# A Strassen FFN on one Trainium2 core: more gate and up pairs by seven products, part of the elementwise work on GpSimd

## The chip, the core and the metric

The kernel runs on one core of one Trainium2 chip. The metric is the device time of one execution in microseconds; three executions of the kernel before took 948.73, 949.64 and 949.51 us (median 949.51). Five engines work side by side, each through its own instructions in order: TensorE (PE, matmuls, with weight loads shown as PEld), VectorE (DVE), ScalarE (ACT), GpSimd (POOL) and SyncE (SP), which here only issues transfers. ACT and POOL issue transfers too, from the same in-order streams as their arithmetic.

## What is computed

Two decoder layers on one sequence of 512 tokens of width 1024, in float32. Each layer is a token mixer (layer 0 a pooling mixer, layer 1 a differential attention), a residual with LayerNorm, a SwiGLU FFN of inner width 2816, and a residual with LayerNorm again:

```python
def _swiglu(x, w_gate, w_up, w_down):
    return (jax.nn.silu(x @ w_gate) * (x @ w_up)) @ w_down

def reference(x, ...):
    for i in range(DEPTH):            # DEPTH = 2
        h = _multiscale_pool(...) if i % 2 == 0 else _diff_attention(...)
        x = _layernorm(ALPHA * x + h, ln_mix_g[i], ln_mix_b[i])
        x = _layernorm(ALPHA * x + _swiglu(x, w_gate[i], w_up[i], w_down[i]), ln_ffn_g[i], ln_ffn_b[i])
    return x
```

The change concerns the gate and up products of both FFNs and the elementwise work around them.

## The kernel before, in words

**Exact products from rounded halves.** TensorE takes its operands in a rounded float32 form. So every operand is cut in two: ScalarE casts it (the high half), VectorE subtracts the cast from the original (the low half, called a low below), and a product is three matmuls: high by high, high by low, low by high. `split` (L107) does this for activations; in the FFN, `advance` (L555 to L577) does it for weights, with the cast at L569 and the low at L572.

**Weights.** All weights lie in DRAM in rows of 128x1024 (512 KB). `fetch` (L95) and `refill` have SyncE load them into five raw buffers; `advance(upto)` casts and subtracts ahead of the products, into six pairs of weight buffers. The steps of this work are listed by hand per pair (L528 to L545).

**The gate stage.** The inner width is 22 blocks of 128, taken as eleven pairs (k, k + 11). A *plain* pair multiplies gate and up weights of both blocks with all 512 tokens: 4 weight rows, 96 matmuls of 512 columns. A *Strassen* pair (`SPLIT`, pairs 4 to 10; `strassen`, L778) sees the pair as a 2x2 product of halves (tokens by halves of the 1024 input features) and makes seven half-size products P1, Q5, P6, Q3, P7, P2, Q4 instead of eight: 24 matmuls of 256 columns each. It needs sums of weight rows (four per pair, VectorE, L566), and sums of x (`xs`, made once by `sums_of_x`, L604). The products accumulate in three PSUM banks A, B and C of eight; between products ScalarE copies or VectorE subtracts from a bank (L829 to L849), and the result is `hid`, the gated hidden activations.

**Start of the gate stage.** Before both halves of the tokens are normalised and transposed, the first blocks (three in layer 0, two in layer 1) are multiplied with tokens 0 to 255 alone, then with tokens 256 to 511. `turn(n, s)` (L234), the transposition of token block s, runs in between; `late` says where.

**Down sums.** The down product is Strassen too. It needs sums of down weight rows: `load_terms` (L658) has GpSimd's queue load a block and add one row to it in flight (the accumulating transfer, L666), `sum_terms` (L669) adds twice on VectorE (128x512 each, L671 and L672) and stores `tsum` through ScalarE's queue. It also needs sums of `hid`: `sum_hidden(k)` (L691) has four additions of 128x256 on VectorE (L697 to L700), a cast on ScalarE (L702), a low of 128x512 on VectorE (L704), and a store `ssum` through ScalarE's queue. Such generators are put in the list `behind`, and `catch_up()` takes one step of each after every product. `affine` (L203) applies the LayerNorm's gain and bias to the residual rows (two VectorE operations of 128x1024 for each of four token blocks).

Nothing is scheduled by a tool: each engine's order is the order of the calls.

Of the kernel before, what the change touches and what calls it, by code (L numbers as in the profile page):

```python
# [12 lines left out]
F32 = mybir.dt.float32  # L13
# [3 lines left out]
ALU = mybir.AluOpType  # L17
# [31 lines left out]
SPLIT = (4, 5, 6, 7, 8, 9, 10)  # L49
# [5 lines left out]
def trunk(ctx, tc, x, wall, pscale, lam_p, subln, table, lng, lnb, band, first, onehot, out):  # L55
# [37 lines left out]
    total = wall.shape[0]  # L93

    def fetch(upto):  # L95
        while fetched[0] < min(upto, total):
            c = fetched[0]
            raws[c] = keep.tile([P, 1024], F32, tag="raw", name=f"raw{c}", bufs=RAWS)
            nc.sync.dma_start(out=raws[c], in_=wall[c])
            fetched[0] += 1  # L100
# [133 lines left out]
    def turn(n, s):  # L234
        transposed(n, s)
        turned(n, s)
# [226 lines left out]
    def ffn(layer, late):  # L463
        n = 2 * layer + 1
        final = n == 2 * DEPTH - 1
        c0 = base[0]
        c1 = c0 + 2 * FB
        tt = nc.vector.tensor_tensor
        with tc.tile_pool(name=f"ffn{layer}", bufs=1) as fp:
# [7 lines left out]

            order = [k + j * HALF for k in range(HALF) for j in range(2)]
# [3 lines left out]
            def block(i, b):  # L482

                if PAIRS[i][1] == 2:
                    return wall[c1 + 4 * i + b]
                return wall[c1 + 20 + b // 2][:, (b % 2) * 512 : (b % 2 + 1) * 512]
# [32 lines left out]

            chunks, index, steps = [], {}, []  # L520
# [7 lines left out]
            for k in range(HALF):  # L528
                j0 = index[k] = len(chunks)
                c = c0 + 4 * k  # L530
                if k in SPLIT:

# [3 lines left out]
                    for w in (  # L536
                        "low 0, sum 1, cast 1, sum 4, cast 3, cast 4, low 1, sum 2, cast 2, low 3, "
                        "low 2, sum 6, cast 5, cast 6, low 4, low 5, low 6"
                    ).split(", "):
                        steps.append((w[:-2], j0 + int(w[-1])))  # L540
                else:
                    for i in range(4):
                        chunks.append((c + i, ()))
                        step("cast", j0 + i)
                        step("low", j0 + i)  # L545
# [11 lines left out]
            def advance(upto, strict=False):  # L557

                upto = min(upto, len(chunks))
                while not all(j in finished for j in range(upto)):  # L560
                    kind, j = steps.pop(1 if strict and steps[0][1] >= upto else 0)
# [8 lines left out]
                    else:  # L570
                        h, l = halves[j]
                        tt(l, t, h.bitcast(F32), op=ALU.subtract)  # L572
# [32 lines left out]

            def sums_of_x():

                r0, r1, r2, r3 = spare(4), spare(15), spare(6), spare(17)

                def whole(t, a, b):  # L610
                    tt(t, quarter(a, 0, b).bitcast(F32), quarter(a, 1, b).bitcast(F32), op=ALU.add)
# [7 lines left out]
                whole(r2, 0, 0)  # L619
                yield  # L620
                whole(r3, 0, 1)
                yield
                whole(r0, 1, 0)
                whole(r1, 1, 1)
                yield
# [3 lines left out]
                high(2, r0)  # L629
                yield  # L630
                tt(r2, r1, r2, op=ALU.subtract)  # L631
                high(1, r2)
                low(0, r1)
# [3 lines left out]
                low(2, r0)  # L637
                yield
# [12 lines left out]

            def load_terms(k):
                if k < HALF - 1:
                    c = c1 + 4 * (k // 2)
                    src = wall[c : c + 4][:, :, term_slice(k)].rearrange("(j r) p t -> p j r t", j=2)
                else:
                    src = wall[c1 + 20 : c1 + 22].rearrange("j p (r t) -> p j r t", r=2)
                if k == 1:  # L658
                    t = rows_of[:, :, 4:6, :]
                elif k % 2 == 0 and k < HALF - 1:  # L660
                    t = rows_of[:, :, 9:11, :]
                else:
                    t = keep.tile([P, 2, 2, 512], F32, tag="gb", name=f"b{layer}_{k}")
                for j in range(2):
                    nc.gpsimd.dma_start(out=t[:, j], in_=src[:, j])  # L665
                nc.gpsimd.dma_start(out=t[:, 0], in_=src[:, :, 1], accum_op=ALU.add)  # L666
                terms[k] = t

            def sum_terms(k):  # L669
                t = terms.pop(k)  # L670
                tt(t[:, 1, 1], t[:, 0, 0], t[:, 1, 1], op=ALU.add)  # L671
                tt(t[:, 1, 0], t[:, 1, 1], t[:, 1, 0], op=ALU.add)  # L672
# [4 lines left out]
                if k + 2 < HALF - 1 and k != 1:  # L677
                    load_terms(k + 2)
                if k == HALF - 2:
                    load_terms(HALF - 1)  # L680

            summed_rows = [0]
            behind = []

            def weight_sums():
                g = sum_terms(summed_rows[0])
                summed_rows[0] += 1
                next(g)
                behind.append(g)

            def sum_hidden(k):  # L691
# [8 lines left out]
                tt(u[:, 1, :], u[:, 1, :], second, op=ALU.add)  # L700
# [676 lines left out]
```

## Time and profile before

One profiled execution has a span of 947.3 us from the first to the last instruction, beside the runs' median of 949.51 us.

| what | value |
|---|---|
| span of the profiled execution | 947.3 us |
| PE busy | 934.1 us, 99% |
| DVE busy | 781.3 us, 82% |
| ACT busy | 490.1 us, 52% |
| POOL busy | 108.4 us, 11% |
| PE's share of the chain that ended last | 92% |
| first product of layer 0's gate stage to the first down product | 32.36 to 266.67 us |
| the same in layer 1 | 603.27 to 833.82 us |
| bytes moved | 196.99 MB, mean 208 GB/s |

An engine's row of a timeline gives the start, the time of one instruction (of several equal ones, x2, together), the engine, the line, the operation with output and inputs, and in brackets what it had waited for. Successive instructions overlap a little in it, so that the distance between two starts is the better price of one in a dense stretch. A row of the table by stretches gives each engine's busy time in it, the clock granted to TensorE, the busy share of the transfer engines and what they moved.

### The profile page before, as it was taken

The page shows a single profiled execution, that of the slowest core. Times are in us where ns is not written, and L with a number is a line of the kernel's source. Part 1 is how long each engine was busy: PE and PEld are TensorE (multiplying, and loading weights), DVE is VectorE, ACT ScalarE, POOL GpSimd, SP SyncE. Part 2 cuts the span into 40 slices and gives each one's busy share as a digit, 9 for nine tenths or more (in the row PEclk, how much of TensorE's full clock was granted, in tenths as well). Part 3 has the DMA queues.
Part 4 walks back from the last instruction along what each step waited for, and adds up shares of the span by engine and source line. Part 5 has one row for each costly group of instructions (what it writes and reads, how often), then busy time and mean ns, then how long its engine had stood idle before and what let it go on. Part 6 is the DMA issues. An engine that isn't in the chain of part 4 may idle for free.

```text
span 947.3 us, 15363 instructions
## 1 busy us (share of the span) xinstructions
PE 934.1 (99%) x5976; PEld 845.7 (89%) x5976; DVE 781.3 (82%) x1149; ACT 490.1 (52%) x788; POOL 108.4 (11%) x133
## 2 busy tenths in 40 slices
PE   9999999999999999999999999999999999999996
PEld 8898899999988888988888888998899999988885
DVE  8859879999988777688777677789779999987778
ACT  6752444555564457655566553833345554564450
POOL 4121121110001101000000000211111110001101
PEclk9999999999999999999999999999999999999998
DMA  9387988885888964333233222396888885878952
GB/s 244 125 266 236 341 269 246 265 261 208 255 255 271 363 219 136 95 89 101 78 123 83 64 90 90 118 324 197 262 266 250 255 272 204 261 249 271 356 171 90
DMA packets 82248, 196.99 MB, mean 208 GB/s; under 512 B 14804, under 2 KB 26324, under 8 KB 82174
## 3 DMA queue, kind: packets, MB, share of 16 engines
q1 hardware_dynamic: 42876, 115.07, 36.9%
q0 software_dynamic: 15520, 46.14, 17.8%
q10 hardware_dynamic: 23778, 34.78, 10.2%
q8 instruction: 47, 0.77, 0.3%
q14 instruction: 27, 0.22, 0.1%
HBM read 159.25 MB, written 36.72 MB: 207 GB/s over the span
## 4 chain that ended last, share of the span: by engine, by line
PE 92%; DVE 4%; ACT 2%; issue 1%; POOL 0%; DVEq 0%; POOLq 0%
PE A L820 17%; PE P L886 13%; PE C L820 9%; PE Q L886 6%; PE B L820 4%; PE g L129 3%; PE u L128 3%; PE u L127 3%; PE u L129 3%; PE g L127 3%; PE g L128 3%; PE s L1085 2%; PE v L127 2%; PE v L128 2%; PE v L129 2%; PE q L128 2%
## 5 line engine op out<-in xcount | busy, mean ns | idle before, releaser
L566 DVE TENSOR_TENSOR raw<-raw,raw 128x1024 f32<-128x1024 f32 x56 | 68.3, 1219 | 0.5
L109 ACT CAST xs<-hid 128x512 fp32r<-128x512 f32 (+1 forms) x60 | 34.7, 581 | 24.4 <-DVE hid L734 24.4
L224 ACT ACTIVATE y<-pt,bT,gT 128x128 f32<-128x128 f32 x96 | 36.1, 456 | 20.1 <-PE pt L213 20.1
L110 DVE TENSOR_TENSOR xs<-hid,xs 128x512 fp32r<-128x512 f32 (+1 forms) x60 | 38.5, 644 | 7.8 <-ACT xs L109 7.8
L1095 ACT ACTIVATE p<-p,mn 128x128 f32<-128x128 f32 (+3 forms) x64 | 35.4, 554 | 14.9 <-DVE mn L1090 14.9
L665 POOL DMA_DIRECT2D b<-in_wall x20 | 14.0, 705 | 175.0 <-DVE g_58l L572 66.1
L598 DVE TENSOR_TENSOR hid<-sg,u 128x512 f32<-128x512 f32 x16 | 11.0, 687 | 27.5 <-PE u L129 16.8
L726 POOL DMA_DIRECT2D xs<-ssum x24 | 17.4, 725 | 140.7 <-PE Q L886 119.5
L177 POOL TENSOR_TENSOR rs<-rs,mhalf 128x1 f32<-128x1 f32 x16 | 12.5, 784 | 170.5 <-DVE rs L176 131.0
L110 DVE TENSOR_TENSOR xt<-y,xt 128x512 fp32r<-128x512 f32 x24 | 16.3, 689 | 17.5 <-ACT xt L109 17.5
L1090 DVE CUSTOM_DVE_ANT_0 p<-s,bias 128x128 f32<-128x128 f32 (+3 forms) x64 | 28.1, 485 | 0.0
L665 POOL DMA_DIRECT2D hid<-in_wall x24 | 18.7, 821 | 81.1 <-DMA tsum<-hid 49.4
L110 POOL TENSOR_TENSOR sql<-sq,sqh 128x512 fp32r<-128x512 f32 x7 | 9.0, 1291 | 165.3 <-ACT sqh L109 165.3
L702 ACT CAST v<-u 128x512 fp32r<-128x512 f32 x22 | 13.6, 620 | 26.9 <-DVE u L700 26.7
L168 DVE BATCH_NORM_STATS2 st<-res 128x6 f32<-128x512 f32 x32 | 22.2, 695 | 1.1
L846 ACT ACTIVATE sg<-sg 128x512 f32<-128x512 f32 x14 | 8.9, 633 | 25.7 <-DVE sg L839 25.7
L110 DVE TENSOR_TENSOR heads<-k,heads 128x512 fp32r<-128x512 f32 x8 | 5.5, 692 | 19.9 <-ACT heads L109 19.9
L614 ACT CAST xs<-hid 128x1024 fp32r<-128x1024 f32 x8 | 8.4, 1051 | 24.0 <-DVE hid L631 11.6
L666 POOL DMA_DIRECT2D hid<-in_wall x12 | 14.8, 1232 | 48.2 <-DMA hid<-in_wall 44.9
L835 DVE TENSOR_TENSOR hid<-C,hid 128x512 f32<-128x512 f32 x14 | 9.7, 692 | 10.8 <-PE C L820 9.2
L1109 DVE SCALAR_TENSOR_TENSOR p<-p,sm,p 128x128 f32<-128x128 f32 (+3 forms) x32 | 17.7, 552 | 1.1
L109 ACT CAST heads<-k 128x512 fp32r<-128x512 f32 x8 | 4.7, 589 | 26.0 <-PE k L129 26.0
(1119 smaller groups left out, 3727.7 us busy)
## 6 DMA issues: line engine op xcount, KB each, us to landing
raw<-in_wall SPq DMA_DIRECT2D x122, 512.0 KB, 4.5
r<-tsum SPq DMA_DIRECT2D x40, 512.0 KB, 4.3
hid<-in_wall POOLq DMA_DIRECT2D x36, 512.0 KB, 6.9
b<-in_wall POOLq DMA_DIRECT2D x30, 512.0 KB, 6.4
r<-in_wall SPq DMA_DIRECT2D x30, 512.0 KB, 4.5
tsum<-hid ACTq DMA_DIRECT2D x24, 512.0 KB, 5.3
ssum<-v ACTq DMA_DIRECT2D x22, 512.0 KB, 4.4
tsum<-b ACTq DMA_DIRECT2D x20, 512.0 KB, 5.2
```

The costliest lines, as they stand in the source:

```text
L109: nc.scalar.copy(dst_h, src)
L110: (low or nc.vector).tensor_tensor(dst_l, src, dst_h.bitcast(F32), op=ALU.subtract)
L127: nc.tensor.matmul(acc, ah, bh, start=start, stop=False)
L128: nc.tensor.matmul(acc, ah, bl, start=False, stop=False)
L129: nc.tensor.matmul(acc, al, bh, start=False, stop=stop)
L224: nc.scalar.activation(y[:, k, :], pt[:, k * P : (k + 1) * P], AF.Identity, bias=bT[:, n, kk : kk + 1], scale=gT[:, n, kk : kk + 1],)
L566: tt(t, raws[pair[0]], raws[pair[1]], op=ALU.add)
L665: nc.gpsimd.dma_start(out=t[:, j], in_=src[:, j])
L820: nc.tensor.matmul(o, w[:, c], x[:, kk, :], start=p in ("P1", "Q5", "P2") and f + kk + e == 0, stop=p in ("Q4", "Q3", "P2") and (f, kk, e) ...
L886: nc.tensor.matmul(accs[s], x[:, k, r], y[:, c], start=first and k == 0 and e == 0, stop=last and k == m - 1 and e == 2, skip_group_check= ...
L1090: nc.vector.tensor_tensor_reduce(out=p, in0=accs[c][:, :w], in1=biases[h][:, w - 1 :: -1] if w < S else biases[h][:, ::-1], op0=ALU.add, o ...
L1095: nc.scalar.activation(p, p, AF.Exp, bias=mn[:, q, c : c + 1], scale=-1.0, accum_out=sm[:, q, c : c + 1],)
```

## The change

Ten of the eleven pairs are made by Strassen's scheme; pair 0 alone stays plain. Layer 0 starts with the products P1 and P2 of pairs 1, 2 and 3 (layer 1: pairs 1 and 2), which need only the first token half. These stay in their banks A and B. Then comes plain pair 0, then the started pairs (five products left) in turn with others (seven). Started pairs load their weight rows 0 and 3 twice. `slow`, GpSimd's tensor_tensor, makes now: both additions of each down weight sum, all five operations of `sum_hidden`, both operations of the FFN's four affine steps, the two sums of x over the first token half, and one low of 128x1024 in each started pair and in those others with an index up to 6 (layer 1: up to 4). The two sums of x over the second token half go away: `turn` writes its float32 result there. The accumulating transfer is issued later than the loads it follows.

```diff
-SPLIT = (4, 5, 6, 7, 8, 9, 10)
+SPLIT = tuple(range(1, HALF))
+EARLY = (3, 2)
...
+    def sequence(layer):
+        early = EARLY[layer]
+        first, others = range(1, early + 1), range(early + 1, HALF)
+        return [k for p in zip(first, others) for k in p] + list(others)[early:]
...
-    def turned(n, s):
+    def turned(n, s, kept=None):
         for i, pt in enumerate(turns.pop((n, s))):
-            y = keep.tile([P, 4, P], F32, tag="y", name=f"y{n}_{s}_{i}", bufs=2)
+            if kept:
+                y = kept[i][:, :, s % 2 * P : (s % 2 + 1) * P]
+            else:
+                y = keep.tile([P, 4, P], F32, tag="y", name=f"y{n}_{s}_{i}", bufs=2)
...
+        slow = nc.gpsimd.tensor_tensor
...
+                if k in started:
+                    chunks += [(c, (c, c + 1)), (c, (c, c + 2)), (c + 2, ()), (c + 1, (c + 1, c + 2))]
+                    chunks += [(c, (c, c + 3))]
+                    listed(
+                        j0,
+                        "sum 0, cast 0, cast 2, sum 3, cast 3, low 0, sum 1, cast 1, low 2, "
+                        "low 1, sum 4, cast 4, low 3, low 4",
+                    )
+                    slow_lows |= {j0 + 2}
...
+                    if k <= 2 * early:
+                        slow_lows |= {j0 + 5}
...
-                        tt(l, t, h.bitcast(F32), op=ALU.subtract)
+                        (slow if j in slow_lows else tt)(l, t, h.bitcast(F32), op=ALU.subtract)
...
             def sum_terms(k):
+                for _ in range(4 if k == HALF - 1 else 0):
+                    yield
                 t = terms.pop(k)
-                tt(t[:, 1, 1], t[:, 0, 0], t[:, 1, 1], op=ALU.add)
-                tt(t[:, 1, 0], t[:, 1, 1], t[:, 1, 0], op=ALU.add)
+                slow(t[:, 1, 1], t[:, 0, 0], t[:, 1, 1], op=ALU.add)
+                slow(t[:, 1, 0], t[:, 1, 1], t[:, 1, 0], op=ALU.add)
+                yield
                 yield
                 dst = tsum[:, k // 2, :, term_slice(k)].rearrange("(j r) p t -> p j r t", j=2)
                 for j in range(2):
                     nc.scalar.dma_start(out=dst[:, j], in_=t[:, j])
...
+                yield
+                yield
+                load_terms(following)
+                yield
+                yield
+                yield
+                add_terms(following)
...
-                tt(u[:, 0, :], first, second, op=ALU.subtract)
-                tt(second, second, a22, op=ALU.subtract)
-                tt(u[:, 1, :], a12, first, op=ALU.subtract)
-                tt(u[:, 1, :], u[:, 1, :], second, op=ALU.add)
+                slow(u[:, 0, :], first, second, op=ALU.subtract)
+                slow(second, second, a22, op=ALU.subtract)
+                slow(u[:, 1, :], a12, first, op=ALU.subtract)
+                slow(u[:, 1, :], u[:, 1, :], second, op=ALU.add)
+                yield
                 yield
                 nc.scalar.copy(v[:, :, 0, :], u)
                 yield
-                tt(v[:, :, 1, :], u, v[:, :, 0, :].bitcast(F32), op=ALU.subtract)
+                slow(v[:, :, 1, :], u, v[:, :, 0, :].bitcast(F32), op=ALU.subtract)
...
+            def pool_work():
+
+                def whole(t, b):
+                    slow(t, quarter(0, 0, b).bitcast(F32), quarter(0, 1, b).bitcast(F32), op=ALU.add)
+
+                whole(r2, 0)
+                yield
+                whole(r3, 1)
+                yield
+                add_terms(0)
+                for s in range(SB):
+                    z, gb = res[:, s, :], gbs[n - 1]
+                    slow(z, z, gb[:, 0, :], op=ALU.mult)
+                    yield
+                    slow(z, z, gb[:, 1, :], op=ALU.add)
+                    if s == 1:
+                        add_terms(1)
+                    yield
+
             load_terms(0)
             load_terms(1)
+            side = pool_work()
+            e = 0
+            for k in started:
+                for p in ("P1", "P2"):
+                    b = "A" if p == "P1" else "B"
+                    banks[k, b] = bank(f"{b}{layer}_{k}")
+                    part(banks[k, b], e, p)
+                    if e in late:
+                        turn(n - 1, late[e], (r0, r1))
+                    ahead(e + 6)
+                    next(side, None)
+                    e += 1
...
+            def plain(k):
+                j = index[k]
+                for f in (k, k + HALF):
+                    a = (bank(f"g{layer}_{f}"), bank(f"u{layer}_{f}"))
                     for i in range(2):
+                        product(a[i], j, 0, S)
+                        j += 1
+                        next(sums, None)
+                        ahead(j + 5)
+                        next(side, None)
+                        next(side, None)
                         catch_up()
+                    gated(f, *a)
+                    if f == k:
+                        behind.append(sum_terms(1))
+                behind.append(sum_hidden(k))
...
+            next(sums)
+            behind.append(sum_terms(0))
+            plain(0)
+            for g in (sums, side):
+                for _ in g:
+                    pass
+            for i, k in enumerate(pairs):
+                strassen(k, i + 2)
...
-    ffn(0, {(0, 1): later(0, 2), (1, 0): later(0, 3)})
-    attention(later(1, 3))
-    ffn(1, {(0, 1): later(2, 3)})
+    ffn(0, {1: 2, 2: 3})
+    attention(lambda: turn(1, 3))
+    ffn(1, {0: 2, 1: 3})
```

More of the change, by code (lines that the diff above doesn't have):

```diff
@@ L515, in refill @@
                     held[0] += 1
+            started = list(range(1, early + 1))
+            pairs = sequence(layer)
             chunks, index, steps = [], {}, []
@@ new lines, in strassen @@
+            def strassen(k, following):
+                names = {"P1": "A", "P6": "A", "P7": "A", "Q4": "A", "Q5": "C", "Q3": "C", "P2": "B"}
+                pair = hid[:, k : k + HALF + 1 : HALF, :]
+                first, second = pair[:, :, :256], pair[:, :, 256:]
+                todo = [p for p in GATE if k not in started or p not in ("P1", "P2")]
+                for j, p in enumerate(todo):
+                    if (k, names[p]) not in banks:
+                        banks[k, names[p]] = bank(f"{names[p]}{layer}_{k}")
+                    flat = banks[k, names[p]]
+                    part(flat, index[k] + j, p)
+                    acc = both(flat)
+                    if p == "P1" or j == 0:
+                        g0 = tile_of(k, 0)
+                        nc.scalar.copy(g0, banks[k, "A"])
+                    if k in started and j == 0:
+                        tt(g0, banks[k, "B"], g0, op=ALU.add)
+                    if p == "Q5":
```

241 lines of the change are left out of this document (98 added, 143 removed).

## The prediction

> **What bounds the kernel now.** I read the page first, then busy time by stretches, then the chain that ended last.
>
> ```profile
> span 947.3 us, 15363 instructions
> PE 934.1 (99%) x5976; PEld 845.7 (89%) x5976; DVE 781.3 (82%) x1149; ACT 490.1 (52%) x788; POOL 108.4 (11%) x133
> ```
>
> ```profile
> core 0: us, PE busy (x) PEld busy (x) DVE busy (x) ACT busy (x) POOL busy (x), PEclk, DMA share, GB/s
> 66.00:86.00 20.00, 20.00 (x110) 17.41 (x110) 19.73 (x23) 4.71 (x7) 2.69 (x3) 1.00 1.00 314
> 165.88:186.04 20.16, 20.16 (x170) 20.16 (x170) 19.18 (x24) 10.33 (x13) 2.83 (x4) 1.00 0.93 281
> ```
>
> TensorE is the bound: 99% of the span. The second stretch is one Strassen pair. TensorE never stops, but VectorE is busy 19.18 of 20.16 us and stays just hidden. More Strassen pairs mean less TensorE and more VectorE work; so the question is what GpSimd's help is worth.
>
> ```profile
> 128.43 2.88 PE C L820 x24
> ...
> 266.67 14.99 PE P L886 x66
> 281.66 14.96 PE Q L886 x66
> ...
> 833.82 14.99 PE P L886 x66
> ```
>
> In the chain a product of 24 matmuls of 256 columns takes 2.88 us (0.120 each); 66 matmuls of 512 columns take 14.96 (0.2267 each, not 0.240). So a Strassen pair costs 7 x 2.88 = 20.16, a plain one 96 x 0.2267 = 21.76. The gate stages end at 266.67 and 833.82; they begin here:
>
> ```profile
> 32.36 0.38 PE L127 MATMUL g<-xt,w2h 128*128 128x256 f32 x1 [0.39 <-ACT xt L109]
> ...
> 53.69 0.28 PE L127 MATMUL g<-xt,w2h 128*128 128x256 f32 x1
> ```
>
> ```profile
> 603.27 0.36 PE L127 MATMUL g<-xt,w100h 128*128 128x256 f32 x1
> ```
>
> They last 234.3 and 230.6 us.
>
> **The change, part by part.** *TensorE.* The program has 528 more matmuls of 256 columns and 336 fewer of 512: 528 x 0.120 - 336 x 0.2267 = 63.4 - 76.2 = -12.8 us. A gate stage then needs 10 x 20.16 + 21.76 and two transpositions of about 1.0, 225.4 us. This is all that the change can win.
>
> *Banks in layer 0.* Three started pairs hold six of eight banks; block 0's gate and up take the last two, so block 11's gate waits for block 0's silu. In ScalarE's order two casts stand ahead of that silu, and the first writes a weight buffer that block 0's up product reads to its end.
>
> ```profile
> 52.55 1.28 ACT L597 ACT_TABLE_LOAD   x1
> ...
> 56.77 0.60 ACT L597 ACTIVATE sg<-g 128x512 f32<-128x512 f32 x1 [2.94 <-PE g L129]
> 57.26 1.04 ACT L569 CAST g_6h<-raw 128x1024 fp32r<-128x1024 f32 x1
> ```
>
> TensorE stops for 2 x 1.04 + 1.28 + 0.60 = 4.0 us. Pair 1's first product waits in the same way for a cast and block 11's silu, 1.6. Layer 1 holds four banks and has no such wait. Together +5.6, if nothing longer covers it.
>
> *Work moved to GpSimd.* First VectorE's prices, from a dense part of the Strassen pair, then GpSimd's.
>
> ```profile
> 169.07 0.68 DVE L849 TENSOR_TENSOR hid<-sg,hid 128x512 f32<-128x512 f32 x1
> 169.68 0.69 DVE L671 TENSOR_TENSOR hid<-hid 128x512 f32<-128x512 f32 x1
> ...
> 173.73 1.22 DVE L572 TENSOR_TENSOR g_36l<-raw,g_36h 128x1024 fp32r<-128x1024 f32 x1
> 174.87 1.22 DVE L572 TENSOR_TENSOR g_37l<-raw,g_37h 128x1024 fp32r<-128x1024 f32 x1
> 176.00 0.69 DVE L704 TENSOR_TENSOR v<-u,v 128x512 fp32r<-128x512 f32 x1
> ```
>
> From start to start: 0.60 for 128x512, 1.135 for 128x1024.
>
> ```profile
> 9.85 2.55 POOL L110 TENSOR_TENSOR xt<-res,xt 128x512 fp32r<-128x512 f32 x2 [7.02 <-ACT xt L109]
> 13.90 1.80 POOL L110 TENSOR_TENSOR xt<-res,xt 128x512 fp32r<-128x512 f32 x1 [1.50 <-ACT xt L109]
> 16.32 3.45 POOL L110 TENSOR_TENSOR w2l<-raw,w2h 128x1024 fp32r<-128x1024 f32 x1 [0.61 <-ACT w2h L109]
> ```
>
> ```profile
> 13.32 1.22 DVE L110 TENSOR_TENSOR pw0l<-raw,pw0h 128x1024 fp32r<-128x1024 f32 x1
> 14.46 1.28 DVE L110 TENSOR_TENSOR pooled<-pool,pooled 128x512 fp32r<-128x512 f32 x2
> ...
> 16.25 1.23 DVE L110 TENSOR_TENSOR pw1l<-raw,pw1h 128x1024 fp32r<-128x1024 f32 x1
> 17.39 0.69 DVE L161 SCALAR_TENSOR_TENSOR res<-res,mix 128x512 f32<-128x512 f32 x1
> ```
>
> Undisturbed, GpSimd takes 1.275 for 128x512. The one at 13.90 took 0.53 more: VectorE was in a subtraction with both inputs in SBUF, and GpSimd's end, 15.70, is 1.24 after VectorE had left it (14.46). The one at 16.32 ended at 19.77, 2.38 after VectorE went on from such a subtraction (17.39). While VectorE read one input from PSUM (pool, mix), GpSimd was not held. So GpSimd stands still while VectorE reads two SBUF inputs. Undisturbed prices: 2.38 for 128x1024, and for 128x256, which the trace lacks, 0.72 on the line through both sizes (half of 1.275, 0.64, is the lower bound).
>
> Is VectorE held too while GpSimd works? The nearest rows are an attention operation (L1105) beside GpSimd's low.
>
> ```profile
> 416.66 1.29 POOL L110 TENSOR_TENSOR sql<-sq,sqh 128x512 fp32r<-128x512 f32 x1 [37.94 <-ACT sqh L109]
> ```
>
> ```profile
> 398.39 0.35 DVE L1105 TENSOR_SCALAR p<-p,sm,nlam 128x128 f32<-128x128 f32 x1
> 417.61 0.42 DVE L1105 TENSOR_SCALAR p<-p,sm,nlam 128x128 f32<-128x128 f32 x1
> ```
>
> ```profile
> L1105 DVE TENSOR_SCALAR p<-p,sm,nlam 128x128 f32<-128x128 f32 x8 | 3.3, 412 | 0.3
> ```
>
> Free of GpSimd it takes 0.35. Begun beside GpSimd's low it takes 0.42 and ends at 418.03, 0.08 after GpSimd (417.95). The mean of the eight, 0.412, says that most were late so. It has one SBUF input, so it is kin, not proof: between "not held" and "held until GpSimd ends" I take the second, which its end agrees with.
>
> The Trainium skill ("SBUF — State Buffer", section "Who interferes with whom") states that a VectorE instruction with two SBUF inputs and a GpSimd instruction that reads SBUF exclude each other, for the whole instruction, whoever came first. By that rule moving such work wins nothing and makes it twice as dear; the trace agrees on GpSimd's side (3.45 instead of 2.38), and no run here shows the other side for two inputs. With the page's rule alone the sum below stays as it is.
>
> Then both engines' work of this kind adds up. Per gate stage, layer 0 (layer 1):
> - VectorE: 64 (66) lows, 40 weight sums, 8 operations for the sums of x, 112 (114) x 1.135; 20 gatings and 4 lows of x, 24 x 0.60: 141.5 (143.8).
> - GpSimd: 2 sums of x, 8 affine, 6 (4) lows, 16 (14) x 2.38; 22 down sums and 11 lows of hidden sums, 33 x 1.275; 44 additions x 0.72: 111.9 (107.1).
>
> Sum 253.4 (250.9), against 225.4 of TensorE. VectorE's operations on PSUM, 32 x 0.60, run beside GpSimd and are not counted. Queueing makes it a bound: ScalarE's stores of down sums wait for GpSimd's additions, and behind them in ScalarE's order stand the casts and bank copies that TensorE needs; GpSimd's lows feed TensorE directly. So GpSimd can lag by about one pair: its last hidden sum and down sum, 4 x 0.72 + 3 x 1.275 = 6.7, may fall after the stage. Changing hands costs VectorE the overlap of two instructions, 1.22 - 1.135 = 0.09, at up to 93 (91) operations; I take half, 4.2, as some fall where VectorE waits anyway.
>
> In layer 0 GpSimd begins where it did, with the down loads that follow the pool stage:
>
> ```profile
> 46.40 1.60 POOL L665 DMA_DIRECT2D hid<-in_wall  x2 [4.47 <-ACT xt L109]
> ```
>
> Layer 0 ends at 46.4 + 253.4 - 6.7 + 4.2 = 297.3, 30.6 later; layer 1 takes 250.9 - 6.7 + 4.2 = 248.4 from 603.27, 17.8 longer. The bank wait is covered. 947.3 + 30.6 + 17.8 = 995.7, and the runs' median, 949.51, lies 2.2 above the span of 947.3: 998.
>
> *The rest.* A pair moves ten transfers of 512 KB, 5.2 MB; a started and another pair (34.6 us) 303 GB/s, under the 314 of the first stretch above: nothing. Late loads have about a pair of slack.
>
> **Rivals.** *B, the engines do not hold each other for long:* VectorE runs on. GpSimd has 112 us of work and its issues,
>
> ```profile
> L665 POOL DMA_DIRECT2D hid<-in_wall x24 | 18.7, 821 | 81.1 <-DMA tsum<-hid 49.4 <-DVE g_36l L572 9.5 <-DVE u L700 8.3
> L666 POOL DMA_DIRECT2D hid<-in_wall x12 | 14.8, 1232 | 48.2 <-DMA hid<-in_wall 44.9 <-DMA raw<-in_wall 3.3
> ```
>
> 22 x 0.82 + 11 x 1.23 = 32, 144 of 225. Its first down sum, which ScalarE needs before block 11's silu at 79.4 (53.69 + 4 x 5.44 + 4.0), is ready at 46.4 + 4 x 0.82 + 4.8 + 1.2 + 9.5 + 1.2 + 2.4 + 4.8 + 2.6 = 76.2: in time. Then 947.3 - 12.8 + 5.6 + 2.2 = 942. For it: POOL is busy 11% now, so the time is there. Against: the 3.45 and the 0.42. It decides as soon as VectorE's 128x1024 stay at 1.22 beside GpSimd. *C, one-sided:* GpSimd waits out each VectorE instruction in flight, VectorE is never held. The ten operations before that down sum are late by up to 1.14 each; ScalarE stalls by up to 8 in layer 0 and 6 in layer 1: 942 to 956, middle 949. For it: 13.90 and 16.32 show just this side. Against: 0.42.
>
> **How the numbers follow.** A has 0.65, B 0.21, C 0.14. A's own range: with 0.64 for 128x256 (3.5 a layer) and no changing of hands (4.2), 983; with all of it (4.2) and 5% of each sum idle, as VectorE was in the dense pair (12.6), 1031. The whole range reaches down to B's 942 plus 1, and up to 1025: 943 to 1025 leaves out half of B and A's top. Under 0.2%, 1.9 us, is no change that a measurement of this kernel can tell. Faster: B and 0.03 of C, 0.24; same 0.05 of C; slower: A and 0.06 of C, 0.71.
>
> **What would show it.** Right: in the gate stages VectorE's 128x1024 take well over 1.22 and GpSimd's well over 2.38, their spans alternate, TensorE waits for lows and for ScalarE behind its stores, and the stages last about 265 and 248. Wrong: VectorE's groups keep their means, TensorE's idle time is a few us around plain pair 0 in layer 0, and the stages last about 230 and 225. In both, a Strassen product must keep 2.88.

## The result, and the profile after

The changed kernel takes 1056.92 us (median; 1055.69 to 1058.19) beside 949.58 for the kernel before on the same chip: ratio 1.1131, 95% interval 1.1115 to 1.1147. Slower was forecast, 998 us; the range ended at 1025. The profiled execution has a span of 1056.1 us, 108.8 more than before.

First the page of the changed kernel: span, busy time by engine, and the granted clock in 40 slices.

```profile
span 1056.1 us, 15912 instructions
PE 952.6 (90%) x6168; PEld 868.3 (82%) x6168; DVE 843.0 (80%) x1021; ACT 517.8 (49%) x824; POOL 419.9 (40%) x317
PEclk9985998999999999999999999896989999999999
```

TensorE has 12.8 us less to do (forecast: 934.1 - 12.8 = 921.3) and yet is busy for 952.6: 31.3 us more, in matmuls at a lower granted clock (0.956 on average, 0.997 before). Idle time grew from 947.3 - 934.1 = 13.2 to 1056.1 - 952.6 = 103.5 us. So -12.8 + 31.3 + 90.3 = 108.8. Where it stands, by the chain that ended last (a product of 24 matmuls, and the first down product of each layer):

```profile
119.61 2.88 PE A L816 x24
...
330.05 14.99 PE P L953 x66
...
942.44 14.99 PE P L953 x66
```

A product that nothing disturbs still takes 2.88 us. Layer 0's down stage begins at 330.05 in place of 266.67, 63.4 us later; layer 1's at 942.44 in place of 833.82, a further 45.2. The rest of the kernel is as long as before. Within the gate stages, busy times and granted clock by stretches (start, pair 1's first product, the end of the interleaved pairs, the last four pairs; then layer 1's start):

```profile
core 0: us, PE busy (x) PEld busy (x) DVE busy (x) ACT busy (x) POOL busy (x), PEclk, DMA share, GB/s
32.40:116.50 84.10, 48.78 (x262) 41.52 (x261) 67.27 (x44) 33.40 (x52) 49.95 (x27) 0.78 0.46 148
116.50:242.00 125.50, 108.69 (x840) 107.47 (x840) 96.14 (x79) 52.45 (x68) 87.59 (x63) 0.93 0.77 231
242.00:330.00 88.00, 84.75 (x697) 83.94 (x698) 75.28 (x68) 43.90 (x57) 47.61 (x35) 1.00 0.71 224
667.00:720.00 53.00, 38.23 (x209) 33.64 (x208) 50.86 (x28) 21.01 (x33) 39.64 (x20) 0.88 0.45 129
```

The start is worst: TensorE works 48.78 of 84.10 us, at 0.78 of its clock. In the last stretch it is nearly whole again.

Is VectorE held by GpSimd? Timelines of the two engines in the same microseconds, VectorE first:

```profile
77.03 3.43 DVE L619 TENSOR_TENSOR g_10l<-raw,g_10h 128x1024 fp32r<-128x1024 f32 x1
80.38 3.35 DVE L663 TENSOR_TENSOR hid<-hid 128x1024 f32<-128x1024 f32 x1
```

```profile
79.31 3.33 POOL L838 TENSOR_TENSOR res<-res,gb 128x1024 f32<-128x1024 f32 x1
```

VectorE's 128x1024 take 3.4 us instead of 1.22, GpSimd's 3.33 instead of 2.38. They start alternately, and each instruction's time holds most of one of the other's. VectorE's reads of a bank are not held (group by line, the bank read at 686 ns as before, the weight sums at 1611 ns instead of 1219):

```profile
L613 DVE TENSOR_TENSOR raw<-raw,raw 128x1024 f32<-128x1024 f32 x80 | 128.9, 1611 | 4.2 <-DMA raw<-in_wall 3.2
L902 DVE TENSOR_TENSOR hid<-C,hid 128x512 f32<-128x512 f32 x20 | 13.7, 686 | 29.0 <-PE C L816 26.1
```

The turns are not always one by one. At the start of layer 1, GpSimd's timeline and one VectorE low beside it:

```profile
670.30 2.91 POOL L707 DMA_DIRECT2D hid<-in_wall  x4 [0.25 <-PE pt L232]
673.24 4.84 POOL L829 TENSOR_TENSOR hid<-xt 128x1024 f32<-128x1024 f32 x2
...
678.81 2.79 POOL L838 TENSOR_TENSOR res<-res,gb 128x1024 f32<-128x1024 f32 x1
```

```profile
671.95 10.74 DVE L129 TENSOR_TENSOR w109l<-raw,w109h 128x1024 fp32r<-128x1024 f32 x1
```

One subtraction stood from 671.95 to 682.69 while GpSimd issued transfers and ran three operations, and TensorE waited for it. What TensorE waited for in the whole kernel (microseconds in total, times, longest):

```profile
PE A L816 <- DVE hid L904: 36.2, 20, 4.9
PE g L146 <- ACT sg L644: 23.7, 1, 23.7
PE g L147 <- DVE xt L129: 9.6, 2, 8.5
...
PE B L816 <- DVE w109l L129: 5.7, 1, 5.7
```

Neither of the two largest is in the sum that gave 998: Q4 waits until VectorE has read P7's bank (L904), which the forecast doesn't have, and block 11's gate waits for block 0's silu (L644) to free a bank, 23.7 us where 4.0 was forecast and held to be covered. ScalarE's timeline while TensorE stands, from 77.3 to 101.0 us:

```profile
83.77 1.04 ACT L658 CAST xs<-hid 128x1024 fp32r<-128x1024 f32 x1 [5.52 <-DVE hid L663]
87.05 1.04 ACT L658 CAST xs<-hid 128x1024 fp32r<-128x1024 f32 x1 [2.24 <-DVE hid L666]
91.52 1.04 ACT L616 CAST g_11h<-raw 128x1024 fp32r<-128x1024 f32 x1 [3.42 <-DVE raw L613]
98.02 1.05 ACT L658 CAST xs<-hid 128x1024 fp32r<-128x1024 f32 x1 [5.46 <-DVE hid L670]
```

These four casts stand ahead of that silu, and each waits for a sum that VectorE has yet to make (three sums of tokens, one of weight rows).

### The profile page after: what moved, and what is told of

Same layout as the page of the kernel before. It is cut to its first block, busy times and chain, and to the rows that moved or that the text cites. A ratio compares the mean times of both kernels' runs of the same rounds, so it can differ in the third digit from the quotient of the medians.

```text
span 1056.1 us, 15912 instructions
## 1 busy us (share of the span) xinstructions
PE 952.6 (90%) x6168; PEld 868.3 (82%) x6168; DVE 843.0 (80%) x1021; ACT 517.8 (49%) x824; POOL 419.9 (40%) x317
## 3 DMA queue, kind: packets, MB, share of 16 engines
q0 software_dynamic: 15520, 46.14, 16.4%
## 4 chain that ended last, share of the span: by engine, by line
PE 62%; DVE 21%; issue 6%; ACT 4%; DMA 2%; ACTq 0%; DVEq 0%; POOL 0%; POOLq 0%; SPq 0%
PE A L816 16%; PE P L953 12%; PE C L816 8%; DVE raw L613 6%; PE Q L953 6%; PE s L1152 2%; PE v L146 2%; PE v L147 1%; PE v L148 1%; DMA raw<-in_wall 1%; PE q L147 1%; PE q L148 1%; PE q L146 1%; PE k L146 1%; PE k L148 1%
## 5 line engine op out<-in xcount | busy, mean ns | idle before, releaser
L613 DVE TENSOR_TENSOR raw<-raw,raw 128x1024 f32<-128x1024 f32 x80 | 128.9, 1611 | 4.2 <-DMA raw<-in_wall 3.2
L744 POOL TENSOR_TENSOR u<-hid 128x256 f32<-128x256 f32 x22 | 34.4, 1562 | 72.8 <-DVE hid L916 72.7
L752 POOL TENSOR_TENSOR v<-u,v 128x512 fp32r<-128x512 f32 x22 | 43.4, 1974 | 13.7 <-ACT v L750 13.7
L707 POOL DMA_DIRECT2D hid<-in_wall x32 | 24.9, 787 | 32.1 <-DMA tsum<-hid 26.7
L902 DVE TENSOR_TENSOR hid<-C,hid 128x512 f32<-128x512 f32 x20 | 13.7, 686 | 29.0 <-PE C L816 26.1
L246 ACT ACTIVATE y<-pt,bT,gT 128x128 f32<-128x128 f32 x64 | 24.1, 455 | 17.4 <-PE pt L232 17.3
L745 POOL TENSOR_TENSOR hid<-hid 128x256 f32<-128x256 f32 x22 | 30.8, 1399 | 2.2 <-DVE hid L645 0.6
L900 ACT COPY hid<-A 128x512 f32<-128x512 f32 x20 | 11.7, 587 | 38.9 <-PE A L816 36.6
L712 POOL DMA_DIRECT2D hid<-in_wall x16 | 19.7, 1228 | 26.5 <-DMA hid<-in_wall 18.3
L719 POOL TENSOR_TENSOR hid<-hid 128x512 f32<-128x512 f32 x16 | 29.2, 1825 | 1.3
L909 ACT ACTIVATE sg<-A 128x512 f32<-128x512 f32 x20 | 11.7, 587 | 35.6 <-PE A L816 35.6
L746 POOL TENSOR_TENSOR u<-hid 128x256 f32<-128x256 f32 x22 | 29.0, 1318 | 0.0
L718 POOL TENSOR_TENSOR hid<-hid 128x512 f32<-128x512 f32 x16 | 27.0, 1690 | 0.0
L913 ACT ACTIVATE sg<-sg 128x512 f32<-128x512 f32 x20 | 12.6, 631 | 27.3 <-DVE sg L906 27.3
L146 PE MATMUL g<-xt,g_8h 128*128 128x512 f32 x8 | 4.5, 559 | 23.7 <-ACT sg L644 23.7
```

What stands on the lines that cost most here:

```text
L146: nc.tensor.matmul(acc, ah, bh, start=start, stop=False)
L613: tt(t, raws[pair[0]], raws[pair[1]], op=ALU.add)
L719: slow(t[:, 1, 0], t[:, 1, 1], t[:, 1, 0], op=ALU.add)
L744: slow(u[:, 0, :], first, second, op=ALU.subtract)
L745: slow(second, second, a22, op=ALU.subtract)
L752: slow(v[:, :, 1, :], u, v[:, :, 0, :].bitcast(F32), op=ALU.subtract)
```

## The experiments

Three theories stood. T: the engines exclude each other where both read SBUF, and the added load is the whole loss. R1: ScalarE's queue, stores ahead of casts and silus. R2: banks and the order of the products. R3, a merely slow GpSimd, had fallen with the 3.4 us rows above. In the tables, each ratio is to the kernel before on the same chip, with its 95% interval.

**1. Back to VectorE, at once and part by part**

```diff
-        slow = nc.gpsimd.tensor_tensor
+        slow = nc.vector.tensor_tensor
```

(everything; in the other three `slow` becomes `tt` at L619 alone, at L829, L838 and L840, or at L718 to L752.)

> Ten Strassen pairs as in the changed kernel, but everything that was moved to GpSimd is back on VectorE. Theory T (GpSimd's reads and VectorE's two-operand instructions take turns, so their work adds; the rest of the loss, starved sums and the lower granted clock, follows from that): with GpSimd idle VectorE carries about 216 us in a gate stage beside TensorE's 225, so TensorE sets the end again: 936 to 960 us, granted clock back to 0.99, TensorE busy near 921. Rival R1 (ScalarE's queue: stores that wait for sums hold up the silus and casts behind them, whoever makes the sums): 990 to 1030. Rival R2 (six banks held through the first products in layer 0 and the bank that each Strassen pair reuses; nothing to do with who adds): at least 1010 us, with the first-products stretch of layer 0 still 80 us long. Rival R3 (GpSimd is only slow, and its results come late; no shared path): like T in the time, but then in the part-by-part runs VectorE's own instructions would keep their 1.14 us.

> As the changed kernel, but the ten 128x1024 lows that GpSimd makes are back on VectorE; the other GpSimd work stays. T: by the prices of the added load, 10 x (2.38 - 1.135) = 12.4 us leave the sum, and a low that TensorE waits for is no longer made by an engine with a queue of other work, so 1030 to 1045 us. R1 and R2: no change beyond 5 us (1052 to 1062). R3: 1020 to 1045.

> As the changed kernel, but the quarter sums and the affine steps at the start of each FFN (20 instructions of 128x1024) are back on VectorE. T: 20 x (2.38 - 1.135) = 25 us leave the sum, and with nothing in a row on GpSimd no VectorE instruction is starved beyond one of GpSimd's, so the first-products stretch of layer 0 (84 us) comes down by 12 to 20 and the whole time to 1005 to 1032. If only the sum counts and no starving: 1030. R1, R2: 1050 to 1060. R3 (VectorE gets 22.7 us more, TensorE waits as long): 1050 to 1080.

> As the changed kernel, but the down weights' sums and the sums of the gated hidden (seven instructions for each of 22 pairs) are back on VectorE; GpSimd keeps the lows, the quarter sums and the affine steps. T: of the added load 22 x (6.7 - 3.1) = 79 us go, more than what lies above TensorE in the steady stretch, so TensorE sets the end there and the loss of the start stays: 970 to 1000 us. R1: 1000 to 1030 (the stores still wait for sums, sooner made). R2: 1040 or more. R3: 975 to 1010.

| on VectorE | us | less than 1056.9 | ratio |
|---|---|---|---|
| everything | 1000.89 | 56.0 | 1.0540 (1.0524 to 1.0556) |
| lows | 1044.49 | 12.4 | 1.1004 (1.0988 to 1.1021) |
| start (sums of x, affine) | 1032.52 | 24.4 | 1.0879 (1.0852 to 1.0906) |
| sums of down weights and hidden | 1035.47 | 21.4 | 1.0894 (1.0871 to 1.0917) |

The parts add up: 12.4 + 24.4 + 21.4 = 58.2 beside 56.0. Lows and start give just what 1.135 instead of 2.38 an instruction promised (12.4 and 25). The sums gave 21 of 79, and 1035.47 lies in no theory's range (T: 970 to 1000). In the pairs most of the added load seems to lie under TensorE's own work. Layer 0's last four pairs in the chain that ended last, first in the changed kernel, then with everything on VectorE:

```profile
242.01 6.02 PE A L816 x48
```

```profile
216.63 5.84 PE A L816 x48
...
300.80 14.99 PE P L953 x66
```

They take 88.0 us (242.01 to 330.05) with GpSimd and 84.2 without, 3.9 of the 29.3 us by which this layer's gate stage differs.

T missed the first run too: with GpSimd out of it, 1001 and not 936 to 960. R2 (at least 1010) missed as well, though part 2 finds what it names among the losses. R1's 990 to 1030 holds this run, but not the lows and the start, for which it had 1050 and more; part 4 tries it by itself. About half of the loss is not the shared path. TensorE's waits with everything on VectorE:

```profile
PE A L816 <- DVE hid L904: 20.9, 9, 4.8
PE g L146 <- ACT sg L644: 17.5, 1, 17.5
```

The same two waits lead. Timelines of ScalarE and then of TensorE in this run, layer 0:

```profile
80.07 1.04 ACT L658 CAST xs<-hid 128x1024 fp32r<-128x1024 f32 x1 [6.15 <-DVE hid L670]
81.13 1.28 ACT L644 ACT_TABLE_LOAD   x1
82.42 0.60 ACT L644 ACTIVATE sg<-g 128x512 f32<-128x512 f32 x1
```

```profile
83.07 0.80 PE L146 MATMUL g<-xt,g_8h 128*128 128x512 f32 x1 [17.49 <-ACT sg L644]
83.67 0.63 PE L147 MATMUL g<-xt,g_8h 128*128 128x512 f32 x1
84.09 0.63 PE L148 MATMUL g<-xt,g_8l 128*128 128x512 f32 x1
...
89.31 0.39 PE L146 MATMUL g<-xt,g_8h 128*128 128x512 f32 x1
...
153.86 0.80 PE L816 MATMUL A<-xt,g_26h 128*128 128x256 f32 x2 [3.75 <-DVE hid L904]
```

The silu stands in ScalarE's order behind a cast that waits for a token sum (L670), and with six banks held TensorE stops for 17.5 us. After it, matmuls of 512 columns start every 0.43 us instead of 0.2267 until about 89 (by stretches, the granted clock is 0.51 from 83 to 89 us and 1.00 from 89 to 92). The second part is pair 2's Q4: P2, which lies between P7 and Q4 in a full pair, has been computed ahead, so Q4 follows P7 on the same bank and waits 3.75 us for VectorE to read it; then come some 3 us of slow matmuls (granted clock 0.50 from 153.86 to 157). The Trainium skill ("TensorE: Matmul & The Clock Gate", section "HAM oscillation — how this bites in real kernels") states that idle gaps of more than about 3.4 us put the array on half its clock until it has worked a while; the trace agrees (0.43 beside 0.2267 after 17.5 us, a granted clock of 0.50 after 3.75).

**2. The two waits, one at a time**

`EARLY = (2, 2)` frees two banks in layer 0. The silu edit moves each silu behind its own gate product:

```diff
...
                         product(a[i], j, 0, S)
+                        gated(f, a[i], i)
                         j += 1
...
-                    gated(f, *a)
```

(the silu for i = 0, the gate times up for i = 1.) The order edit, for pairs with first products ahead:

```diff
+                places = list(range(len(todo)))
+                if k in started:
+                    todo[2:4], places[2:4] = todo[3:1:-1], places[3:1:-1]
...
-                    part(flat, index[k] + j, p)
+                    part(flat, index[k] + places[j], p)
```

> The changed kernel with two pairs' first products ahead in layer 0 in place of three, so four banks are held through plain pair 0 and not six, and block 11 finds two free. TensorE's 23.7 us wait in layer 0 for the silu that frees a bank then has no cause. If that wait is a loss of its own (banks and ScalarE's order): 1028 to 1040 us. If it only stands where VectorE's and GpSimd's added work would make TensorE wait anyway (the port sum through the start): the wait moves to the sums of tokens or to a low, and the time is 1045 to 1057.

> The kernel with everything back on VectorE (1001 us), again with two pairs ahead in layer 0. There the same wait is 17.5 us with no port in it, followed by about 6 us of matmuls at 628 ns in place of 389. Banks and ScalarE's order as a loss of their own: 978 to 988 us. VectorE too full in the start (it has no gap of 2 us from 57 to 91 us): the wait moves to the token sums, 994 to 1003.

> The kernel with everything back on VectorE and three pairs ahead as in the change, but in the plain pair each silu is issued right behind its gate product, ahead of the next token sum's cast, and each gate-times-up right behind its up product. If ScalarE's order makes the wait (the silu stood behind a cast that waited for VectorE until 80.1 us): block 11 starts near 72 instead of 83.1 us and the time is 986 to 993. If VectorE's load makes it: 998 to 1003.

> The kernel with everything back on VectorE (1001 us); in the five pairs whose first products ran ahead, P7 goes before Q3, so that Q3 on its own bank lies between P7 and Q4 on bank A, where the change left nothing because P2 had been taken out. Theory U (Q4 waits for VectorE to read P7's bank with no product to cover it; 3.8 us each time and a lower granted clock for some us after it): the waits of bank A for that subtraction (20.9 us over 9) fall below 6 and the time to 972 to 984 us. Rival (VectorE is full there, 109.5 of 125.5 us, so that the wait moves): 994 to 1003.

> Everything on VectorE, two pairs ahead in layer 0, each silu behind its gate product, and P7 before Q3. If the three losses are apart from each other, 1001 less about 9 (two pairs), 3 to 6 (silu) and 17 to 28 (order): 960 to 973 us. If they share VectorE's work in the start as their one cause: 980 to 990.

> The changed kernel with its work on GpSimd, and the three edits that took 26 us off the kernel with everything on VectorE (two pairs ahead in layer 0, silus behind their gate products, P7 before Q3). If the losses by the port and the losses by banks and order lie one behind the other: 1057 - 26 = 1031 us, within 5. If the port's load fills the same time (VectorE and GpSimd together are the bound, and TensorE waits for them wherever the banks let it): 1040 to 1055. If the edits save more where every wait is longer: 1015 to 1025.

| kernel | us | change | ratio |
|---|---|---|---|
| changed, two pairs ahead | 1040.53 | -16.4 | 1.0961 (1.0943 to 1.0980) |
| on VectorE, two pairs ahead | 991.62 | -9.3 | 1.0446 (1.0430 to 1.0461) |
| on VectorE, silu first | 995.23 | -5.7 | 1.0483 (1.0468 to 1.0499) |
| on VectorE, P7 before Q3 | 981.11 | -19.8 | 1.0337 (1.0320 to 1.0354) |
| on VectorE, all three | 974.82 | -26.1 | 1.0264 (1.0249 to 1.0280) |
| changed, all three | 1034.83 | -22.1 | 1.0903 (1.0887 to 1.0919) |

Order is the clear one: bank A's waits with P7 before Q3,

```profile
PE g L146 <- ACT sg L644: 17.6, 1, 17.6
...
PE A L816 <- DVE hid L907: 4.7, 5, 2.2
```

are 4.7 us in place of 20.9 (L907 is the old L904), and the time falls by 19.8. Freeing the bank wins about half of its 17.5 us: with the silu first, block 11 starts at 71.6, as expected, but bank A then waits 10.4 us for ScalarE's copies and 24.6 for VectorE. The two runs fell between their two expectations, and so, by half a microsecond, did the changed kernel with two pairs ahead; the wait is partly its own and partly VectorE's load. All three edits came out 2 us above the range for three separate losses (960 to 973): two pairs ahead and the silu treat the same wait, so that the single gains, 34.8 together, overlap.

The last row: in the changed kernel the three edits save 22.1 us, so as a whole these losses lie beside those of the shared path, and 1034.83 - 974.82 = 60.0 is again GpSimd's part. For the single edits this does not hold. Two pairs ahead save 16.4 there (9.3 on VectorE), and silu and order together only 5.7 more (16.8 on VectorE). In TensorE's waits, Q4's fall from 30.9 to 19.9 us with these two, but those for ScalarE's copy of a bank with P1 grow from 11.6 to 34.4: with GpSimd in play, most of what the order saves comes back as another wait.

**3. Who holds whom, by itself.** Eight stretches behind the last output of the kernel before, both engines released together.

> The kernel before, with eight short stretches behind its last output, started together on both engines; its outputs stay as they are and its time grows by 80 to 150 us. (1) VectorE 4 adds of two SBUF tiles 128x1024 alone, (2) GpSimd 4 such adds alone, (3) VectorE 8 with GpSimd 4, (4) VectorE 8 with GpSimd 12 of 128x256, (5) VectorE 12 adds 128x512 with one operand in a bank with GpSimd 4, (6) VectorE 12 one-operand copies 128x1024 with GpSimd 4 adds, (7) VectorE 8 adds with GpSimd 4 one-operand copies, (8) VectorE 8 adds with GpSimd 4 memsets. T: (1) 4.6, (2) 9.5, (3) the sum 8 x 1.14 + 4 x 2.38 = 18.6, taken in turns one by one; (4) the sum 9.1 + 12 x 0.72 = 17.7; (5) the longer, 9.5, each VectorE add at 0.69; (6) the longer, 9.5, or the sum, which decides whether one operand holds too; (7) and (8) open: the sum if GpSimd's writes hold VectorE, the longer if they don't. Rival (no shared path): (3) 9.5, (4) 9.1, each at its own price. Rival (GpSimd waits only): VectorE's adds keep 1.14 in (3) and (4).

VectorE's timeline, stretches 1 and 3 to 8, then GpSimd's in 2 to 6:

```profile
950.34 5.00 DVE L1295 TENSOR_TENSOR pv<-pa,pb 128x1024 f32<-128x1024 f32 x4
966.64 18.12 DVE L1295 TENSOR_TENSOR pv<-pa,pb 128x1024 f32<-128x1024 f32 x8
985.58 12.86 DVE L1295 TENSOR_TENSOR pv<-pa,pb 128x1024 f32<-128x1024 f32 x8
1003.02 8.63 DVE L1295 TENSOR_TENSOR pv<-pa,pq 128x512 f32<-128x512 f32 x12
1013.54 16.77 DVE L1295 COPY pv<-pa 128x1024 f32<-128x1024 f32 x12
1031.14 12.90 DVE L1295 TENSOR_TENSOR pv<-pa,pb 128x1024 f32<-128x1024 f32 x8
1044.86 10.04 DVE L1295 TENSOR_TENSOR pv<-pa,pb 128x1024 f32<-128x1024 f32 x8
```

```profile
956.26 9.58 POOL L1295 TENSOR_TENSOR pg<-pb,pc 128x1024 f32<-128x1024 f32 x4
966.75 13.15 POOL L1295 TENSOR_TENSOR pg<-pb,pc 128x1024 f32<-128x1024 f32 x4
985.68 16.54 POOL L1295 TENSOR_TENSOR pg<-pb,pc 128x256 f32<-128x256 f32 x12
1003.12 9.63 POOL L1295 TENSOR_TENSOR pg<-pb,pc 128x1024 f32<-128x1024 f32 x4
1013.65 11.02 POOL L1295 TENSOR_TENSOR pg<-pb,pc 128x1024 f32<-128x1024 f32 x4
```

(The whole took 1057.71 us with these stretches.) Eight additions beside four of GpSimd's take 18.12, near the sum 10.0 + 9.58 and far from the longer; beside twelve of 128x256 both are done after 16.6, where T's sum was 17.7. Both wait (18.12 instead of 10.0, 13.15 instead of 9.58), so "GpSimd waits only" falls, as does "no shared path". With an operand in a bank neither is held (8.63 for 12, 9.63). Beside GpSimd's one-operand copies VectorE's eight take 12.90, beside its memsets 10.04, which is twice the 5.00 of four alone: it is GpSimd's reads that hold, not its writes. For additions with two SBUF inputs, with one in a bank, and for GpSimd's reads and writes this is as the Trainium skill has it ("SBUF — State Buffer", section "Who interferes with whom"), which the prediction could show on one side only.

**4. What is left on VectorE, and ScalarE's stores**

> As the kernel with three edits, and the eight affine steps of each layer, which nothing waits for before the down stage, go one after each Q3 and P7 of the first four Strassen pairs in place of the start, where VectorE has no gap. If VectorE's load in the start is what is left of the loss: 9 us of its work leave each start, 6 to 16 us less than the kernel with three edits. If the start is bound by the chain through the token sums and ScalarE alone, or the later pairs are as full: within 3 us of it.

> The kernel on VectorE with three edits and the affine steps later (970 us), but again with three pairs ahead in layer 0 and six banks held. If block 11's wait for a bank came from VectorE's load ahead of the silu, it is gone with the affine steps, and the 5 us wait for the last transposed tokens goes too: 962 to 969 us. If six banks cost by themselves: 972 to 982.

> The changed kernel (1057 us), with the stores of the down weights' sums and of the split hidden sums issued by GpSimd's queue, which made these sums, and not by ScalarE's. Rival R1 (casts and silus stand behind a store that waits for GpSimd): 1020 to 1040 us. T: nothing of weight waited there, and GpSimd issues 54 transfers more: 1050 to 1070.

> The kernel before with eight Strassen pairs in place of seven; no pair ahead, nothing on GpSimd, the plain pairs still at the start. TensorE's work falls by 12.8 / 6 = 2.1 us in each layer. If Strassen pairs in their full order (P2 between P7 and Q4) are bound by TensorE: 945 to 947 us. If VectorE is the bound in a Strassen pair as such: 949 to 956.

> The kernel before with nine Strassen pairs; the token sums must end one plain block sooner. TensorE's work falls by 4.3 us in each layer. If only TensorE bounds: 941 to 943 us. If the token sums are late for the first Strassen pair, as VectorE has no gap at the start: 948 to 962.

> The kernel with eight pairs (955 us), with the store of the split hidden sums issued by GpSimd's queue instead of ScalarE's. In eight pairs ScalarE stood 3.6 us before a silu behind that store, which waited for VectorE's low, and TensorE then 3.7 us for the copy of bank A, with slower matmuls after it. If this order on ScalarE's queue is the loss (R1, here with nothing on GpSimd): 946 to 949 us, at or below the kernel before. If VectorE, which has no gap there, is the bound: 953 to 956.

> As the one with the hidden sums' store moved, and the stores of the down weights' sums go to GpSimd's queue too. They had nothing to wait for in the stretch in question, so the same as that within 2 us, 944 to 950, if R1 holds there; 953 to 956 if VectorE is the bound.

The edits: in the first row the affine generator is stepped behind Q3 and P7 of `pairs[:4]`, with the second accumulating transfer issued ahead of all affine steps; in the second `EARLY = (3, 2)` again. In the kernel before, `SPLIT` goes from 3 or from 2 on (for nine, the token sums are finished ahead of the first Strassen pair). The stores:

```diff
-                    nc.scalar.dma_start(out=dst[:, j], in_=t[:, j])
+                    nc.gpsimd.dma_start(out=dst[:, j], in_=t[:, j])
...
-                nc.scalar.dma_start(out=ssum[:, :, :, k, :], in_=v.bitcast(F32))
+                nc.gpsimd.dma_start(out=ssum[:, :, :, k, :], in_=v.bitcast(F32))
```

(Both are moved in the changed kernel and in the last row, the second alone in the row before that.)

| kernel | us | ratio |
|---|---|---|
| on VectorE, three edits, affine later | 970.40 | 1.0221 (1.0205 to 1.0236) |
| the same, three pairs ahead | 975.12 | 1.0275 (1.0257 to 1.0294) |
| changed, stores on GpSimd's queue | 1063.34 | 1.1212 (1.1180 to 1.1245) |
| before, eight pairs | 955.23 | 1.0061 (1.0047 to 1.0074) |
| before, nine pairs | 976.93 | 1.0300 (1.0281 to 1.0320) |
| eight pairs, hidden sums' store on GpSimd | 955.93 | 1.0055 (1.0041 to 1.0069) |
| eight pairs, all these stores on GpSimd | 963.38 | 1.0140 (1.0121 to 1.0159) |

Nine pairs, and eight with all stores moved, came out above both of their expectations. R1, as far as it blames the stores, falls twice: without them in ScalarE's queue nothing is won. In eight pairs it looked strong, since a silu stood 3.6 us behind such a store. With the store moved the silu came as late (111.96 beside 112.14), but the start of that profiled execution was 3.6 us later already (block 11's silu at 92.27 beside 88.71); so what speaks against R1 there are the times, 955.93 beside 955.23. Six banks cost 4.7 us still with the affine steps out of the way. The affine steps in the start cost 4.4, less than the 6 expected.

Eight and nine pairs have no product ahead and none of these additions on GpSimd, and 4.3 and 8.5 us less on TensorE, and still take 0.6% and 3.0% longer than the kernel before. TensorE's waits with nine:

```profile
PE C L820 <- DVE xs L617: 15.8, 2, 7.9
PE C L820 <- ACT xs L614: 10.3, 2, 7.6
```

26.1 us for the sums of tokens, with 27.3 us more time. VectorE makes them in the start, between lows and sums for pairs that now come sooner; in layer 0 its timeline has no gap above 1.2 us from 59.6 to 105. So the ninth pair asks VectorE for its sums before it has room. For the eighth the trace shows only one wait of 3.7 us. No version tried beats the kernel before.

## Why the prediction was wrong in size

The direction held, and one half of the mechanism: the engines exclude each other where both read SBUF, and VectorE alternates with GpSimd. The other half of the loss, 51 us beside 56, was not in the forecast.

- **The price of the shared path was right in size; that it is exact is luck.** The forecast put it as A less B, 998 - 942 = 56 us; everything back on VectorE takes off 56.0, by layer 29.3 and 26.1 (down stages at 300.80 and 887.07 in place of 330.05 and 942.44) where the forecast's parts give 30.6 + 6.4 - 5.6 = 31.4 and 17.8 + 6.4 = 24.2. But the same exchange is worth 48.9 with two pairs ahead and 60.0 with all three edits, and B is a kernel in which GpSimd works without holding anyone, not one with its work on VectorE. Its prices of 2.38 and 1.135 stand in the lows' 12.4 and the start's 24.4 us.
- **The step that failed is "The bank wait is covered"**, and with it the sum that took only the larger load of a stage (layer 0 from 46.4 on; 5.6 for banks in B's 942). Without the path the kernel takes 1001, not 942: the miss of 59 lies in that number. The bank wait is one term of it, the next two points are others. The bank wait, put at 4.0, is 17.5 without GpSimd and 23.7 with it, because ScalarE's casts ahead of the silu wait for VectorE's sums of tokens and weight rows; only two casts' own time, the table load and the silu had been counted. It does not hide under the load: in the changed kernel, two pairs ahead save 16.4 us.
- **A wait was not in the sum at all.** Computing P2 ahead takes away what lay between P7 and Q4: 19.8 us without GpSimd; with it the order was not tried alone, and order and silu together gave 5.7.
- **The clock was not in the sum.** The mean granted clock was 0.997 before and is 0.956 now; the waits brought 31.3 us of slower matmuls in the changed kernel. Each of the savings above holds its share of this.
- **TensorE's -12.8 was never to be had by itself.** 949.5 - 12.8 = 936.7; the best version with ten pairs reaches 970.4. Of the 1000.9 - 936.7 = 64.2 us lost without the shared path, the three edits explain 26.1 and the affine steps 4.4. The trace of that best version places the remaining 33.7 (35.2 in the profiled execution): TensorE's matmuls take 12.5 us more than 921.3, and it idles 22.7 us more than before, as bank A waits 8.7 for VectorE's subtraction and 6.6 and 2.7 for ScalarE's copies, and a gate product 4.9 for the last tokens. VectorE is busy for 88.71 of the 90 us from 90 to 180 there, and nine pairs lose by its sums too. That its work is the cause for ten is argued and not shown, as no run took it away. Nor could B itself be built, GpSimd working beside a VectorE that it doesn't hold: part of the 59 is VectorE's own extra work.
- **Handoffs and lag** (4.2 and 6.7) were not measured apart; the one starved low of 10.74 us is larger than either. "About 265 and 248" became 297.7 (32.4 to 330.05) and 275 us.
- **ScalarE's stores** were named as what queueing binds; they were not.

## What to carry to other kernels

Loads on a shared path and a bank wait can add, as they did here in the start: a sum over a stage is a lower bound, and each wait that the change creates has to be traced back through the queue of the engine that ends it. Before an operation is moved ahead, see what it separated: here P2 gave VectorE the time to read the bank that the next product writes. And where TensorE has never waited, price a wait with the slow matmuls that follow it, 1.7 us after 3.75 here (two products in 7.46 instead of 5.76 in the chain of the run on VectorE):

```profile
153.86 7.46 PE A L816 x48
```

## What the hardware showed beside this

- GpSimd can take several turns in a row: one VectorE subtraction lasted 10.74 us instead of 1.22, through three of GpSimd's operations. In the probe, twelve VectorE copies with a single SBUF operand ended after 16.77 us, and GpSimd's four additions after 11.02 instead of 9.58, so copies seem to be held too; their time alone was not measured.
- After a wait of 17.5 us TensorE needed about 6 us to come back to full spacing, after 3.75 about 3 us. The length of the wait does not settle it: in the run with eight pairs and the hidden sums' store moved, a wait of 3.07 us and one of 0.84 close behind it were followed by slow matmuls up to 119.3, some 6 us from the first wait's end (granted clock 0.51 from 113 to 119.3).
